# Layer 0 of a hybrid streaming encoder: the second block's norm behind the first block's gates, the third block's in front of its own

## Chip, cores and metric

The kernel runs on one NeuronCore of one Trainium2 chip. The metric is the device time of one execution in microseconds (us); lower is better. The runs before the change took 2411.01 to 2415.98 us, with a median of 2411.66 us over 3 runs.

## What is computed

Two layers of a chunk-causal encoder on 1024 prompt frames and 8 x 16 sample frames, together 1152 tokens of width 1024. Cut to what matters:

```
for l in range(2):
    h = rms_norm(x, norm1_g[l])
    q, k, v, a, b = split(h @ w_in[l]);  u = a * sigmoid(b)      # u: the "gates"
    A = sink_attention(rope(norm(q)), rope(norm(k)), v)          # a chunk of 64 reads up to 3 chunks
    C = silu(layer_norm(causal_depthwise_conv31(u)))
    x = x + concat(beta_a * A, beta_c * C) @ w_out[l]
    x = x + relu(rms_norm(x, norm2_g[l]) @ w_up[l])**2 @ w_down[l]
```

## The kernel before

**Blocks.** The tokens lie in three blocks of 384 columns (b = 0, 1, 2), stored with the width on the partitions: a block x is 8 tiles of 128 x 384, loaded by `load_x` (L187) in four DMAs. `rmsnorm` (L250, steps L255) squares x on ScalarE (L260), adds the squares on VectorE (L264, L265), sums over partitions on TensorE (L241), takes the reciprocal root on GpSimd (five short operations, L231 to L235), spreads it with TensorE (L247), and then scales x on VectorE (L275) and parts each value into a rounded half (ScalarE, L276) and a rest (VectorE, L277). The two halves are the tile pair `h`. Every product of a block reads its `h`.

**Products.** Each weight tile arrives as two DMAs `raw`, is rounded on ScalarE (L205) and split on GpSimd (L206), and goes through 24 matmuls of 128 x 384 (L213 to L215). `raw` has 4 buffers, the split weights `w` 6, the PSUM banks `g` of the products 3.

**Stages of layer 0.** `glu(l, b, h)` (L290) makes the gates of block b in eight products; L308 to L310 on ScalarE and L312 on GpSimd finish them. `make_qkv` (L356) makes queries, keys and values in six. `attention` gives a generator that makes one chunk of 64 queries at each step: scores on TensorE (L525), row maximum and its bookkeeping on VectorE (L492 to L502), exponentials (L533) and scaling (L541) on ScalarE, transposes (L550), copies out of PSUM (L551 ScalarE, L552 VectorE), products with the values (L560), and the output `ao` (L564 to L566). The transposes of a chunk and its output share a single PSUM bank `m`, the scores have one tile `s`. `conv` makes the depthwise convolution as 31 VectorE steps (L345, L347) for each of four channel tiles, and its tail (L647 to L665, L640, L641) gives `co`. Attention and convolution advance a little after each product (`tick`). `out(b)` (w_out) multiplies `ao` and `co` with the output weights, and needs all of both.

**What sets the order.** The program is written by hand in this order, and a scheduler then makes one fixed queue for each engine from it at build time, working on its own estimate of the times. On the chip each engine takes its queue strictly in order. Names like `x_573` carry a serial number that shifts by a constant where a tile is made earlier or later; tiles of block 3's norm are x_573, f_578 and following, h_607, h_608 in the kernel before, and x_2223, f_2228 and following, h_2257, h_2258 in the changed one.

Of the kernel before, what the change touches and what calls it, by code (L numbers as in the profile page):

```python
# [42 lines left out]
G1, G2, QG, KG = 0, 8, 16, 17  # L43
# [18 lines left out]
class Kernel:  # L62
# [951 lines left out]
    def run(self):  # L1014
        nc, tc, a = self.nc, self.tc, self.a
        pool = tc.tile_pool
        PS = bass.MemoryType.PSUM
        src = [a["x"][b] for b in range(NB)]
        early = ExitStack()
        self.fp = early.enter_context(pool(name="f0", bufs=1))  # L1020
        self.hp = early.enter_context(pool(name="hp0", bufs=1))
        self.aux = early.enter_context(pool(name="aux0", bufs=1, space=PS))
        x = [self.load_x(src[0])]
        self.load_consts()
        x.append(self.load_x(src[1]))
        h1 = [self.rmsnorm(x[b], 0, G1) for b in range(2)]
        for l in range(DEPTH):
            self.u, self.co, self.k, self.vb = [None] * NB, [None] * NB, [], []
            x, h, ao = [None] * NB, [None] * NB, [None] * NB
            fin = l == DEPTH - 1  # L1030
            nsrc = [a["y"][b] if fin else self.dp.tile([128, KT, BT], F32, tag=f"x{b}", name=f"xd{l}{b}") for b in range(NB)]
            kept = self.dp.tile([128, KT, BT], F32, tag=f"kept{l}", name=f"kept{l}")
            nh = []
            alone, pair, place, mix, conv, att = (t[l] for t in (ALONE, PAIR, PLACE, MIX, CONV, ATT))

            def blk(b, end=False, x=x, h=h, nsrc=nsrc, nh=nh, l=l, fin=fin):
                then = None if fin or not end else lambda: nh.append(self.rmsnorm(x[b], l + 1, G1))
                return x[b], h[b], nsrc[b] if end else None, then

            def attention(b, qf):  # L1040
                ao[b], g = self.attention(l, b, *qf)
                self.side("attention", g, att[b])

            def out(b):
                co = self.tail_of(b)
                x[b] = self.load_x(src[b], self.mark)
                self.w_out(l, x[b], ao[b], co)
                if b < NB - 1:
                    h[b] = self.rmsnorm(x[b], l, G2)

            with tc.tile_pool(name=f"ap{l}", bufs=1) as self.ap:
                self.mix = 0
                self.mix = mix[0]
                self.glu(l, 0, h1[0], conv)
                if l == 0:
                    for n in ("sk", "sv", "sc"):
                        self.after(nc.sync.dma_start(a[n + "o"], a[n + "old"]), self.mark)
                    h1.append(self.rmsnorm(self.load_x(src[2]), l, G1))
                attention(0, self.make_qkv(l, 0, h1[0]))
                if l:  # L1060
                    self.glu(l, 1, h1[1], conv)
                qf = self.make_qkv(l, 1, h1[1])
                self.finish("attention")
                attention(1, qf)
                if not l:
                    self.glu(l, 1, h1[1])
                    self.side("conv", self.conv(l, 1), conv[1])
                if l:
                    out(0)
                    self.flush()  # L1070
                    self.mix = 0
                    self.glu(l, 2, h1[2])
                else:
                    self.glu(l, 2, h1[2])
                    out(0)
                self.back, self.mix = self.feed_forward(l, range(alone), [blk(0)]), mix[1]
                qf = self.make_qkv(l, 2, h1[2])
                self.finish("attention")
                attention(2, qf)
                self.side("conv", self.conv(l, 2), conv[2])  # L1080
                out(1)
                self.flush()
                for _ in self.feed_forward(l, range(alone), [blk(1)], True):
                    pass
                for _ in self.feed_forward(l, range(alone, place), [blk(0), blk(1)]):
                    pass
                self.finish("attention")
            yp = ExitStack()
            self.yp = yp.enter_context(pool(name=f"yp{l}", bufs=1, side="right"))
            forms, three, fourth = self.pair_forms(h[0], h[1])  # L1090
            self.side("forms", three, FORMS[l])

            def firsts(l=l, fourth=fourth):
                self.finish("forms")
                self.side("forms", fourth, 1)

            self.back, self.mix = self.feed_forward(l, range(place, pair), [blk(b) for b in range(2)], then=firsts), mix[2]
            out(2)
            for i in range(0, KT, 4):
                nc.sync.dma_start(kept[:, i:i + 4], x[2][:, i:i + 4])  # L1100
            self.queue = self.quads(l, range(pair, NG))
            self.ahead = self.quad(next(self.queue))
            self.flush()
            self.finish("forms")
            self.mix = 0

            def second(x=x, h=h, l=l):
                x[2] = self.load_x(kept, self.mark)
                self.arena = [self.slot([4, 2, BT], F32, "f"), 0]
                for i, h[2] in enumerate(self.rmsnorm_steps(x[2], l, G2)):  # L1110
                    for _ in range((3, 3, 1)[i]):
                        yield
                self.arena = None

            early.close()
            self.aux = None
            with pool(name=f"xp{l}", bufs=1) as self.xp, pool(name=f"px{l}", bufs=1, space=PS) as self.px:
                self.ahead("sums")
                self.turn = 7
                then = second()  # L1120
                self.pair_feed(l, range(pair, NG), x, forms, then)
                for _ in then:
                    pass
            yp.close()
            early = ExitStack()
            self.fp = early.enter_context(pool(name=f"f{l + 1}", bufs=1))
            self.hp = early.enter_context(pool(name=f"hp{l + 1}", bufs=1))
            self.aux = early.enter_context(pool(name=f"aux{l + 1}", bufs=1, space=PS))
            for b in range(2):
                for i in range(0, KT, 4):  # L1130
                    nc.sync.dma_start(nsrc[b][:, i:i + 4], x[b][:, i:i + 4])
            if fin:
                with tc.tile_pool(name=f"fp{l}", bufs=NFW) as fp:
                    for _ in self.feed_forward(l, range(NG), [blk(2, True)], True, fp):
                        pass
            else:
                self.back = self.feed_forward(l, range(NG), [blk(2, True)])
                self.fill(FILL)
                nh += [self.rmsnorm(x[b], l + 1, G1) for b in range(2)]
            h1, src = nh, nsrc  # L1140
        early.close()
# [119 lines left out]
```

## Time and profile before

| what | value |
|---|---|
| median of 3 runs | 2411.66 us |
| profiled execution, its own time | 2407.56 us |
| span of its instructions | 2405.8 us |
| busy: TensorE (PE), its weight loads | 96 %, 94 % of the span |
| busy: VectorE (DVE), GpSimd (POOL), ScalarE (ACT) | 69 %, 64 %, 53 % |
| mean granted TensorE clock | 0.992 of 2.4 GHz |

The profile is of one execution, 4.1 us under the median of the runs. The shares are means over stages that have different limits. Layer 0 up to the first feed-forward product is about the first 345 us, and it is in this stretch that the change works.

### The profile page before, as it was taken

Reading aid. Unit: us, or ns where it says so; the run is one execution under the profiler, and the core shown is the slowest. Engines: PE = TensorE matmul, PEld = TensorE weight load, DVE = VectorE, ACT = ScalarE, POOL = GpSimd, SP = SyncE. Lnnn points to the kernel's source line nnn. Section 1 sums busy time; section 2 is a strip of 40 time slices with the busy share of each in tenths; the row PEclk is TensorE's granted clock in tenths of the full one; section 3 lists DMA queues with packets and bytes.
Section 4 is the critical chain, followed back from the end, with each engine's and each line's share of the span. In section 5 each row is a group of like instructions: output and inputs, shape, how many; then the busy total and the mean of one; then the engine's idle time right before and its main releaser. Section 6 shows DMA issues by size and latency. Waiting matters only on the chain.

```text
span 2405.8 us, 38983 instructions
## 1 busy us (share of the span) xinstructions
PE 2319.9 (96%) x13822; PEld 2254.8 (94%) x13822; DVE 1658.2 (69%) x2993; ACT 1270.5 (53%) x2732; POOL 1530.3 (64%) x1375
## 2 busy tenths in 40 slices
PE   6999898999999999999999999999999999999999
PEld 6898798999998999999999999999999899999999
DVE  4999887996368777686687764599834877752222
ACT  5467555555435555554566467466443555544442
POOL 5885566566467666766865776856445666676662
PEclk9999899999999999999999999999999999999999
DMA  5422433334332222544333344334333122244442
GB/s 179 139 92 93 122 96 110 111 107 138 110 97 78 68 71 80 164 122 134 101 119 108 114 155 134 128 105 124 97 101 118 55 70 75 84 162 136 132 127 75
DMA packets 164260, 266.49 MB, mean 111 GB/s; under 512 B 24753, under 2 KB 55729, under 8 KB 164017
## 3 DMA queue, kind: packets, MB, share of 16 engines
q1 hardware_dynamic: 164064, 264.01, 35.5%
q8 instruction: 108, 1.77, 0.3%
q14 instruction: 88, 0.71, 0.1%
HBM read 250.19 MB, written 16.05 MB: 111 GB/s over the span
## 4 chain that ended last, share of the span: by engine, by line
PE 76%; DVE 16%; POOL 3%; issue 2%; DMA 2%; ACT 2%; SPq 0%; DVEq 0%; POOLq 0%; ACTq 0%
PE g L715 14%; PE g L213 13%; PE g L215 13%; PE g L214 13%; DVE c L347 5%; PE x L998 4%; PE x L918 4%; PE g L998 3%; PE g L918 2%; PE m L715 2%; PE r L715 2%; POOL w L885 1%; PE c L715 1%; DMA A<-in_w 1%; PE s L525 1%
## 5 line engine op out<-in xcount | busy, mean ns | idle before, releaser
L206 POOL TENSOR_TENSOR w<-raw,w 128x512 fp32r<-128x512 f32 x728 | 965.6, 1336 | 592.3 <-ACT w L205 572.7
L205 ACT CAST w<-raw 128x512 fp32r<-128x512 f32 x728 | 445.6, 620 | 457.6 <-PE g L715 134.6
L213 PE MATMUL g<-h,w 128*128 128x384 f32 x1696 | 576.4, 340 | 7.2 <-ACT h L276 3.8
L214 PE MATMUL g<-h,w 128*128 128x384 f32 x1696 | 573.1, 338 | 1.1 <-DVE h L277 1.1
L215 PE MATMUL g<-h,w 128*128 128x384 f32 x1696 | 573.4, 338 | 0.0
L347 DVE SCALAR_TENSOR_TENSOR c<-u,vec,c 128x384 f32<-128x384 f32 (+1 forms) x960 | 498.5, 519 | 19.0
L715 PE MATMUL g<-hid,w 128*128 128x384 f32 x2304 | 431.2, 341 | 9.3 <-DVE x L717 6.3
L715 PEld LDWEIGHTS g<-hid,w 128*128 128x128 f32 x2304 | 399.6, 189 | 17.8 <-DVE x L717 10.8
L213 PEld LDWEIGHTS g<-h,w 128*128 128x128 f32 x1696 | 320.8, 189 | 11.4 <-ACT h L276 4.6
L214 PEld LDWEIGHTS g<-h,w 128*128 128x128 f32 x1696 | 320.6, 189 | 2.8 <-DVE h L277 2.0
L215 PEld LDWEIGHTS g<-h,w 128*128 128x128 f32 x1696 | 320.4, 189 | 0.7
L699 DVE TENSOR_TENSOR hid<-t,hid 128x384 fp32r<-128x384 f32 x128 | 106.3, 831 | 197.4 <-ACT hid L698 197.2
L885 POOL TENSOR_TENSOR w<-S,w 128x512 fp32r<-128x512 f32 x96 | 138.5, 1446 | 120.0 <-ACT w L884 119.7
L717 DVE TENSOR_TENSOR x<-x,g 128x384 f32<-128x384 f32 x240 | 129.8, 549 | 77.0 <-PE g L715 76.7
L696 ACT ACTIVATE t<-g 128x384 f32<-128x384 f32 x128 | 62.9, 491 | 143.7 <-PE g L215 142.5
L998 PE MATMUL x<-F,w 128*128 128x384 f32 x624 | 119.2, 336 | 3.4 <-DVE x L1001 2.4
L885 POOL TENSOR_TENSOR w<-raw,w 128x512 fp32r<-128x512 f32 x64 | 90.6, 1416 | 41.0 <-ACT w L884 39.7
L998 PEld LDWEIGHTS x<-F,w 128*128 128x128 f32 x624 | 109.4, 188 | 4.9 <-DVE x L1001 2.5
L998 PE MATMUL g<-F,w 128*128 128x384 f32 x528 | 108.3, 340 | 4.1 <-ACT F L807 1.4
L884 ACT CAST w<-S 128x512 fp32r<-128x512 f32 x96 | 59.7, 622 | 96.1 <-DVE S L871 51.1
L998 PEld LDWEIGHTS g<-F,w 128*128 128x128 f32 x528 | 92.6, 188 | 8.4 <-ACT F L807 2.7
L885 POOL TENSOR_TENSOR w<-A,w 128x512 fp32r<-128x512 f32 x64 | 87.0, 1364 | 18.6 <-ACT w L884 18.4
(227 smaller groups left out, 4016.8 us busy)
## 6 DMA issues: line engine op xcount, KB each, us to landing
raw<-in_w SPq DMA_DIRECT2D x792, 256.0 KB, 2.7
A<-in_w SPq DMA_DIRECT2D x64, 256.0 KB, 2.8
x<-in_x SPq DMA_DIRECT2D x24, 384.0 KB, 4.8
x<-xd SPq DMA_DIRECT2D x12, 384.0 KB, 5.2
kept<-x SPq DMA_DIRECT2D x4, 768.0 KB, 4.0
x<-kept SPq DMA_DIRECT2D x8, 384.0 KB, 4.7
xd<-x SPq DMA_DIRECT2D x4, 768.0 KB, 3.5
out_y<-x SPq DMA_DIRECT2D x4, 768.0 KB, 4.7
```

The costliest lines, as they stand in the source:

```text
L205: nc.scalar.copy(u[:, 0], raw)
L206: nc.gpsimd.tensor_tensor(out=u[:, 1], in0=raw, in1=u[:, 0].bitcast(F32), op=ALU.subtract)
L213: nc.tensor.matmul(ps, lhsT=u(0, k), rhs=h(0, k), start=k == 0, stop=False)
L214: nc.tensor.matmul(ps, lhsT=u(0, k), rhs=h(1, k), start=False, stop=False)
L215: self.pe = nc.tensor.matmul(ps, lhsT=u(1, k), rhs=h(0, k), start=False, stop=k == KT - 1)
L347: t = nc.vector.scalar_tensor_tensor(out=o, in0=src(k), scalar=w, in1=o, op0=ALU.mult, op1=ALU.add)
L699: nc.vector.tensor_tensor(out=hid[:, 1], in0=f, in1=hid[:, 0].bitcast(F32), op=ALU.subtract)
L715: self.pe = nc.tensor.matmul(ps, lhsT=u(p), rhs=hid[:, q], start=i == 0, stop=i == n - 1)
L717: nc.vector.tensor_tensor(out=x[:, m], in0=x[:, m], in1=ps, op=ALU.add)
L885: nc.gpsimd.tensor_tensor(out=u[:, 1], in0=f[n], in1=u[:, 0].bitcast(F32), op=ALU.subtract)
L918: nc.tensor.matmul(ps, lhsT=u[:, p, k], rhs=H[h](q, k), start=start and k == 0 and i == 0, stop=k == 3 and i == 2, skip_group_check=True)
L998: nc.tensor.matmul(o, lhsT=u[:, p, 2 * i + j], rhs=F(j, hn)[:, q], start=start and n == 0, stop=n == 5, skip_group_check=True)
```

## The change

Before, blocks 0 and 1 are loaded and normed at the very start, and block 2 is loaded and normed between block 0's gates and its queries. After, only block 0 is normed at the start; block 1 is loaded and normed between block 0's gates and its queries; and block 2 is loaded (its DMAs ordered behind the last sigmoid of block 1's gates) and normed right in front of its own gates. Nothing is added or left out.

```
@@ run @@
         x = [self.load_x(src[0])]
         self.load_consts()
-        x.append(self.load_x(src[1]))
-        h1 = [self.rmsnorm(x[b], 0, G1) for b in range(2)]
+        h1 = [self.rmsnorm(x[0], 0, G1)]
...
                 self.glu(l, 0, h1[0], conv)
                 if l == 0:
...
-                    h1.append(self.rmsnorm(self.load_x(src[2]), l, G1))
+                    h1.append(self.rmsnorm(self.load_x(src[1]), l, G1))
                 attention(0, self.make_qkv(l, 0, h1[0]))
...
                 else:
+                    h1.append(self.rmsnorm(self.load_x(src[2], self.mark), l, G1))
                     self.glu(l, 2, h1[2])
                     out(0)
```

**First place: GpSimd at the start of the program.** `s_118` to `s_122` before, and `s_113` to `s_117` after, are the reciprocal root of block 0's norm; the `w` are the first weights of its gates. Before:

```order
L231 TENSOR_TENSOR s_120<-s_118,half 128x3
L206 TENSOR_TENSOR w_216<-raw_215,w_216 128x512
L232 TENSOR_TENSOR s_121<-s_120,s_118 128x3
L206 TENSOR_TENSOR w_221<-raw_220,w_221 128x512
L206 TENSOR_TENSOR w_250<-raw_249,w_250 128x512
L233 TENSOR_TENSOR s_121<-s_121,s_120 128x3
L206 TENSOR_TENSOR w_255<-raw_254,w_255 128x512
L206 TENSOR_TENSOR w_305<-raw_304,w_305 128x512
L234 TENSOR_SCALAR s_121<-s_121 128x3
L206 TENSOR_TENSOR w_310<-raw_309,w_310 128x512
L235 TENSOR_TENSOR s_122<-s_121,s_120 128x3
```

After, on the same engine at the same place:

```order
L206 TENSOR_TENSOR w_160<-raw_159,w_160 128x512
L206 TENSOR_TENSOR w_165<-raw_164,w_165 128x512
L206 TENSOR_TENSOR w_194<-raw_193,w_194 128x512
L206 TENSOR_TENSOR w_199<-raw_198,w_199 128x512
L206 TENSOR_TENSOR w_249<-raw_248,w_249 128x512
L231 TENSOR_TENSOR s_115<-s_113,half 128x3
L206 TENSOR_TENSOR w_254<-raw_253,w_254 128x512
L232 TENSOR_TENSOR s_116<-s_115,s_113 128x3
L233 TENSOR_TENSOR s_116<-s_116,s_115 128x3
L234 TENSOR_SCALAR s_116<-s_116 128x3
L235 TENSOR_TENSOR s_117<-s_116,s_115 128x3
```

Six splits stand among the five root operations before; after, five of them stand ahead of the root and one inside it. In SyncE's queue, block 1's four load DMAs move from ahead of the first weight to behind the tenth.

**Second place: TensorE at the end of block 1's gates.** `g_2130` before, and `g_2074` after, is the last product of those gates; `g_2282` is the first product of block 2's gates. Before:

```order
L525 MATMUL s_1718<-k_854,q_631 128x192 x12
L214 MATMUL g_2130<-h_183,w_2171 128x384
L215 MATMUL g_2130<-h_182,w_2171 128x384
L213 MATMUL g_2130<-h_182,w_2171 128x384
L214 MATMUL g_2130<-h_183,w_2171 128x384
L215 MATMUL g_2130<-h_182,w_2171 128x384
L213 MATMUL g_2282<-h_607,w_2285 128x384
L214 MATMUL g_2282<-h_608,w_2285 128x384
L215 MATMUL g_2282<-h_607,w_2285 128x384
L213 MATMUL g_2282<-h_607,w_2285 128x384
```

After:

```order
L214 MATMUL g_2074<-h_552,w_2115 128x384
L215 MATMUL g_2074<-h_551,w_2115 128x384
L550 MATMUL m_1583<-cst,p_1555 128x128
L550 MATMUL m_1583<-cst,p_1556 128x128
L525 MATMUL s_1925<-k_798,q_981 128x128 x6
L525 MATMUL s_1925<-k_1302,q_981 128x64 x6
L525 MATMUL s_1925<-k_798,q_981 128x128 x6
L525 MATMUL s_1925<-k_1302,q_981 128x64
L560 MATMUL m_1583<-pt_1576,v_809 128x256 x6
L560 MATMUL m_1583<-pt_1584,v_891 128x256 x3
L525 MATMUL s_1925<-k_1302,q_981 128x64 x5
L550 MATMUL m_1635<-cst,p_1615 128x128
```

After, no product follows block 1's gates for 184 instructions: they are 96 of scores, 30 transposes, 45 with the values and 13 of norms, that is all six chunks of block 1's attention as far as their scores go. Only then comes `g_2282`. Before, these same instructions stand scattered between the products of block 2's gates and of `out(0)`. From the first addition of block 0's down-projection on (L717 into x_2764), the queues of the two kernels differ by exchanged neighbours alone, and from TensorE's instruction 2870 of 13494 on not at all.

**Third place: ScalarE, where block 2's norm stands after the change.** `p_2818` and `p_2819` are the exponentials of block 1's fifth chunk, `p_2621` those of its fourth:

```order
L260 ACTIVATE f_2230<-x_2223 128x768
L533 ACTIVATE p_2621,s_2628<-s_2607,s_2622,s_982 128x3x64 x2
L551 CAST pt_2203<-m_2202 128x256
L260 ACTIVATE f_2233<-x_2223 128x768
L541 ACTIVATE p_2620<-p_2620,s_2628 128x3x64 x2
L541 ACTIVATE p_2621<-p_2621,s_2628 128x3x64 x2
L260 ACTIVATE f_2236<-x_2223 128x768
L533 ACTIVATE p_2818,s_2826<-s_2805,s_2820,s_982 128x3x64 x2
L565 CAST ao_1722<-og_2217 128x4x64
L551 CAST pt_2486<-m_2485 128x512
...
L276 CAST h_2257<-f_2259 128x768
L276 CAST h_2257<-f_2264 128x768
```

Before, the same squares stand among block 0's last gate operations:

```order
L205 CAST w_693<-raw_692 128x512
L260 ACTIVATE f_578<-x_573 128x768
L308 COPY t_551<-g_480 128x384
L205 CAST w_698<-raw_697 128x512
L276 CAST h_182<-f_199 128x768
L205 CAST w_737<-raw_736 128x512
L260 ACTIVATE f_580<-x_573 128x768
```

The squares of block 2's norm now stand behind the exponentials of block 1's fourth chunk, and the halves `h` that its gates need behind the exponentials of the fifth.

## Rows read from the trace of the kernel before

**Rows 1.** Page, busy us (share of the span) and instructions of each engine.
```profile
PE 2319.9 (96%) x13822; PEld 2254.8 (94%) x13822; DVE 1658.2 (69%) x2993; ACT 1270.5 (53%) x2732; POOL 1530.3 (64%) x1375
```

**Rows 2.** Stretch: us, busy PE, PEld, DVE, ACT, POOL; granted clock, DMA share, GB/s.
```profile
61.00:134.00 73.00, 68.06 (x448) 64.45 (x447) 68.14 (x122) 34.61 (x73) 63.48 (x68) 0.93 0.42 136
182.00:230.00 48.00, 46.87 (x311) 44.14 (x310) 46.72 (x86) 32.63 (x89) 25.33 (x22) 1.00 0.30 94
230.00:286.00 56.00, 47.61 (x275) 44.50 (x274) 49.51 (x93) 33.84 (x80) 28.49 (x31) 0.91 0.46 130
286.00:349.00 63.00, 57.56 (x359) 54.59 (x357) 55.59 (x103) 33.51 (x73) 38.36 (x44) 0.92 0.29 89
```

**Rows 3.** Timeline of the start: start us, length us, instruction, idle before and releaser.
```profile
13.02 2.56 ACT L205 CAST w<-raw 128x512 fp32r<-128x512 f32 x4 [3.35 <-DMA raw<-in_w]
13.10 0.86 POOL L231 TENSOR_TENSOR s<-s,half 128x3 f32<-128x3 f32 x1 [10.23 <-DMA raw<-in_w]
13.93 1.26 POOL L206 TENSOR_TENSOR w<-raw,w 128x512 fp32r<-128x512 f32 x1
21.74 0.19 POOL L235 TENSOR_TENSOR s<-s,s 128x3 f32<-128x3 f32 x1
24.98 1.33 PE L213 MATMUL g<-h,w 128*128 128x384 f32 x3 [2.09 <-ACT h L276]
```

**Rows 4.** DMA issues of the first 30 us: what, queue, count, KB each, us to landing.
```profile
x<-in_x SPq DMA_DIRECT2D x8, 384.0 KB, 5.7
```

**Rows 5.** One microsecond of the start, columns as in rows 2.
```profile
11.00:12.00 1.00, 0.70 (x4) 0.70 (x4) 0.25 (x1) 0.00 (x0) 0.00 (x0) 1.00 1.00 377
```

**Rows 6.** TensorE's waits from 60 to 134 us: sum, times, longest.
```profile
PE r L418 <- DVE t L383: 2.1, 1, 2.1
PE g L213 <- DVE s L438: 1.8, 1, 1.8
```

**Rows 7.** Four microseconds behind the first of these waits, columns as in rows 2.
```profile
100.00:104.00 4.00, 2.16 (x8) 2.11 (x8) 3.94 (x9) 1.32 (x3) 2.31 (x3) 0.50 0.09 32
```

**Rows 8.** Timeline of VectorE, 84 to 98 us.
```profile
85.31 2.18 DVE L275 SCALAR_TENSOR_TENSOR f<-x,vec,r 128x384 f32<-128x384 f32 x4
...
96.92 0.54 DVE L383 TENSOR_TENSOR t<-t,r 128x384 f32<-128x384 f32 x1
```

**Rows 9.** Timeline: TensorE's first gate product of block 2, and a chunk on ScalarE.
```profile
182.46 0.34 PE L213 MATMUL g<-h,w 128*128 128x384 f32 x1
...
188.78 0.51 ACT L533 ACTIVATE p<-s,s,s 128x192 f32<-128x192 f32 x1 [2.71 <-DVE s L495]
...
192.36 1.50 ACT L541 ACTIVATE p<-p,s 128x192 f32<-128x192 f32 x4 [0.24 <-DVE s L502]
```

**Rows 10.** ScalarE by form, 100 to 340 us: count, busy us, mean ns, idle before.
```profile
L533 ACT ACTIVATE p<-s,s,s 128x192 f32<-128x192 f32 x40 | 20.3, 512 | 19.9 <-DVE s L495 17.5 <-PE m L550 2.5
L551 ACT CAST pt<-m 128x512 fp32r<-128x512 f32 x11 | 6.4, 583 | 0.1
L260 ACT ACTIVATE f<-x 128x768 f32<-128x768 f32 x4 | 3.4, 845 | 0.0
L665 ACT ACTIVATE u<-u,vec 128x384 f32<-128x384 f32 x4 | 2.5, 696 | 0.4 <-DVE u L662 0.4
L665 ACT ACT_TABLE_LOAD x1 | 1.3, 1283 | 0.0
```

**Rows 11.** TensorE and VectorE by form, 182 to 349 us.
```profile
L560 PE MATMUL m<-pt,v 128*128 128x256 f32 x81 | 12.1, 295 | 0.2 <-DVE pt L552 0.2
...
L525 PE MATMUL s<-k,q 64*128 64x192 f32 x48 | 5.3, 330 | 0.0
...
L492 DVE TENSOR_REDUCE s<-s 128x4 f32<-128x768 f32 x7 | 6.6, 949 | 0.0
```

**Rows 12.** TensorE's longest wait from 134 to 345 us.
```profile
PE g L213 <- ACT co L640: 5.1, 1, 5.1
```

**Rows 13.** Timeline of VectorE: the instruction from which on the queues agree.
```profile
345.44 0.54 DVE L717 TENSOR_TENSOR x<-x,g 128x384 f32<-128x384 f32 x1
```

More of the change, by code (lines that the diff above doesn't have):

```diff
@@ L1024, in run @@
         self.load_consts()
-        x.append(self.load_x(src[1]))
-        h1 = [self.rmsnorm(x[b], 0, G1) for b in range(2)]
+        h1 = [self.rmsnorm(x[0], 0, G1)]
         for l in range(DEPTH):
@@ L1057, in run @@
                         self.after(nc.sync.dma_start(a[n + "o"], a[n + "old"]), self.mark)
-                    h1.append(self.rmsnorm(self.load_x(src[2]), l, G1))
+                    h1.append(self.rmsnorm(self.load_x(src[1]), l, G1))
                 attention(0, self.make_qkv(l, 0, h1[0]))
@@ L1073, in run @@
                 else:
+                    h1.append(self.rmsnorm(self.load_x(src[2], self.mark), l, G1))
                     self.glu(l, 2, h1[2])
```

## The prediction

> **What bounds the kernel now.** I read the page first: TensorE is busy 96 % of the span and its weight loads 94 % [rows 1], so for most of the kernel only TensorE's lost time can be won. Then I cut the part that the change touches into stretches and took, for each, TensorE's lost time as length less busy time x granted clock, since a matmul at half the clock counts as busy. From 61 to 134 us (queries, keys and values of blocks 0 and 1) 73 - 68.06 x 0.93 = 9.7 us are lost; from 182 to 230 us (block 2's gates) 1.1; from 230 to 286 us (`out(0)`) 56 - 47.61 x 0.91 = 12.7; from 286 to 349 us 63 - 57.56 x 0.92 = 10.0 [rows 2]. The reader should see that in all of these VectorE is nearly as busy as TensorE: 68.14 of 73, 46.72 of 48, 49.51 of 56, 55.59 of 63. It is a stage with two limits, and it runs well only where attention and convolution have products of another block beside them. Then I went to the lost time itself: the timeline of the start, the waits, and the granted clock behind a wait. Before 25 us there is one more hole: TensorE's first product starts at 24.98 [rows 3].
>
> **What the change does, part by part.** The work is the same to the last instruction. So every cost or gain is waiting that goes or comes, and I follow TensorE's time to the place from which the queues agree again, the addition at 345.44 [rows 13], about where TensorE reaches 349 us.
>
> *Start.* Before, block 1's four loads of 384 KB lie ahead of the first weight [rows 4]. The DMA engines are full at 377 GB/s [rows 5], so 4 x 0.393 MB take 4.2 us, and the first weight, rounded at 13.02 [rows 3], can be rounded at 8.8. GpSimd then splits from about 9.5. Before, its root began at 13.10 and, with six splits among its steps, ended at 21.93 [rows 3]. After, five splits of 1.26 us come first (to 15.8), then the root's first step of 0.86, a split, and four short steps of 0.19: 18.7. That is 3.2 us earlier; I take **-3** (bounds -2 and -4). Block 1's loads now start when the sixth split has freed its buffer, about 18 us, and land in some 6 us [rows 4], about when ScalarE first wants them behind block 0's last halves. This move costs nothing; if the loads were 2 us late, ScalarE's squares would be, and those have block 0's remaining gates as cover.
>
> *Queries, keys and values.* Block 2's norm held VectorE between 85.31 and 96.92, right ahead of L383, the norm of block 0's keys [rows 8]. TensorE waited 2.1 us for L383 and then 1.8 us for L438 behind it [rows 6], and the granted clock stood at 0.50, that is 1.2 GHz, right behind the first wait [rows 7]: some 3 us more. Block 1's norm now stands there instead of two norms, so VectorE reaches L383 with some 11 us less work done (the stretch 85.31 to 96.92). I take 7 of the 9.7 us: **-7** (bounds 0 and -9.7).
>
> *The hole in front of block 2's gates.* Now block 2's norm starts only when block 1's gates are done, and its squares and halves stand on ScalarE behind the exponentials of block 1's fourth and fifth chunk. Products before 182.46 [rows 9] have nothing to follow them but attention, chunk after chunk. I estimate the hole from block 1's last gate product to block 2's first. From the first gate product of block 2 to the exponentials of block 0's last chunk before: 188.78 - 182.46 = 6.3 [rows 9]; I take the same lead. One chunk on ScalarE, first exponential to last scaling: 192.36 + 1.50 - 188.78 = 5.1 [rows 9]; the next chunk's scores, 12 at 0.11 (5.3 / 48), its maximum, 0.95 [rows 11], and a copy out of PSUM, 0.58 [rows 10], come between: 7.9, say 8 a chunk. From those exponentials to the halves of block 2's `h` there are five chunks: 40. The tail of block 0's convolution falls into the same place on ScalarE with two table loads of 1.3 and its SiLU of 2.5, and block 2's squares take 3.4 [rows 10]: 8.5. One more for the first halves: 6.3 + 40 + 8.5 + 1 = 56 us. In them TensorE does 184 small instructions that lay behind 182.46 before, at 0.11 to 0.15 each (5.3 / 48, 12.1 / 81 [rows 11]): 20 to 27, I take 22. So the hole costs 56 - 22 = **+34**. From below, ScalarE's own work alone is 24 x 0.51 + 20 x 0.375 + 6 x 0.58 + 2.5 + 2.6 + 3.4 = 32 [rows 9, 10], with the lead 38, which makes +16. From above, waits let the clock fall to half, as after 2.1 us in rows 7; if half of the 22 us of small matmuls lie on the chain at twice their time, the hole is 67 and the cost +45. Behind TensorE wait its gate products, and with them ScalarE's L308 to L310, the convolution of block 1 (ordered behind block 2's products) and `out(0)`.
>
> *Behind the hole.* Block 1's attention is then over, and block 0's `co`, for which TensorE waited 5.1 us in `out(0)` [rows 12], is long ready. So the 12.7 us lost from 230 to 286 mostly go; of the 10.0 from 286 to 349, where `out(0)`'s own norm is waited for, I let 4 go. Against that, the halves of `h` come one by one while VectorE still has a softmax to do, and the clock must rise again: +4 (an estimate: four microseconds at 0.50 as in [rows 7] cost 2, and I let the halves cost as much). Together 11 + 4 - 4: **-11** (bounds -19 and -4).
>
> Sum: -3 - 7 + 34 - 11 = **+13 us**. The profiled execution took 2407.56 us of device time around its span of 2405.8, so it would take 2420.6. That execution is 4.1 us under the median of the runs; on the median the forecast is 2411.66 + 13 = 2424.7, about **2425 us**.
>
> **A rule against the trace.** The rows show that products and attention beside each other fill TensorE to 46.87 of 48 us [rows 2], and the change takes them apart. The Trainium skill, Perfetto Trace Analysis, section Optimization Strategy, says that where the most contended engine changes between regimes, interleaving the regimes may help; it speaks against this change. By that rule the sum is a loss; without it, by the section Identifying the Most-Contended Engine of the same page, the busiest engine is the one to improve, and an unchanged TensorE at 96 % would leave the sum at 0. The second reading is a rival of its own below.
>
> **The rivals.**
> - *Slower as above* (the forecast), chance 0.62.
> - *Faster: ScalarE fills the hole.* If the six chunks overlap so well that ScalarE is never idle, the hole is 38 us and costs +16; with -9 from the queries and -11 behind the hole, the sum is -3 - 9 + 16 - 11 = -7: 2405 us. It decides below a hole of 43 us (22 + 3 + 7 + 11). For it speaks that two chunks are always in work; against it that scores have one tile, transposes one bank, so each chunk waits for the one ahead, and that ScalarE stood idle 19.9 us ahead of 40 exponentials [rows 10]. Chance 0.13.
> - *No change: waits only move.* Attention's dependencies cost TensorE the same wherever they stand, 33.5 us between 61 and 349 as now (9.7 + 1.1 + 12.7 + 10.0 [rows 2]): 2412 us. The hole's 34 us would have to be just these; but not all of them come from attention. Chance 0.11.
> - *Much slower: hole at half clock.* Hole 67 us, nothing won in the queries, losses behind it down by only 9: -3 + 45 - 9 = +33: 2445 us. Chance 0.14.
> - That block 2's norm is made early all the same is excluded by ScalarE's queue, where its squares stand behind a fourth chunk that needs block 1's queries.
>
> The unknown terms give the likeliest case a range of 2417 to 2436; with the neighbours the range is **2409 to 2443**. A measurement of this kernel tells 0.2 %, 4.8 us, from no change. Faster by more: 0.13. Within: 0.13 (the third case, and a little of the first). Slower: 0.74.
>
> **What would show it.** Right: the first product at about 22 us; no wait for L383 near 95; block 1's gates done near 172; then TensorE busy less than half of the time for 50 to 60 us, with the clock at 0.5 in parts, and ScalarE's exponentials following each other at about 8 us; block 2's gates from about 228; no wait for `co` in `out(0)`; the L717 at about 358. Wrong: a hole under 43 us; a hole that GpSimd or the load of block 2 ends instead of ScalarE; or losses between 290 and 400 us that vanish because TensorE comes later while VectorE does not.

## The result: 21 us slower, and where the profile after shows them

The changed kernel takes 2432.16 us (median of 6 runs, 2428.48 to 2434.87), the kernel before, run on the same chip, 2410.98 us (6 runs, 2407.15 to 2415.98): a ratio of 1.0088, 95 % interval 1.0073 to 1.0103. The forecast was 2425 us with a range of 2409 to 2443. So the direction held and the range held, but the loss is 21 us where 13 were forecast. Between the two profiled executions it is 25.4 us (2432.95 against 2407.56). The page of the changed kernel:

```profile
PE 2331.0 (96%) x13822; PEld 2266.5 (93%) x13822; DVE 1651.7 (68%) x2993; ACT 1273.4 (52%) x2732; POOL 1530.1 (63%) x1375
```

The shares are those of [rows 1] to within a point: the page alone shows nothing. The first three stretches of [rows 2] do:

```profile
61.00:134.00 73.00, 68.96 (x457) 64.77 (x455) 62.79 (x123) 33.14 (x73) 64.10 (x72) 0.93 0.41 134
182.00:230.00 48.00, 30.04 (x152) 23.96 (x152) 24.77 (x58) 33.09 (x90) 6.41 (x10) 0.54 0.19 59
230.00:286.00 56.00, 51.16 (x289) 49.27 (x290) 43.08 (x81) 33.46 (x80) 28.47 (x32) 0.85 0.32 93
```

In the second row TensorE is busy 30 of 48 us at a granted clock of 0.54. That is the hole. TensorE's timeline shows its edges and its beat, in one row for each chunk's scores:

```profile
183.57 0.34 PE L215 MATMUL g<-h,w 128*128 128x384 f32 x1
...
189.31 2.34 PE L525 MATMUL s<-k,q 64*128 64x128 f32 x19 [1.24 <-ACT p L533]
...
198.81 2.61 PE L525 MATMUL s<-k,q 64*128 64x64 f32 x22 [1.03 <-ACT p L533]
...
208.90 1.60 PE L525 MATMUL s<-k,q 64*128 64x192 f32 x12 [1.24 <-ACT p L533]
...
218.69 1.60 PE L525 MATMUL s<-k,q 64*128 64x192 f32 x12 [0.97 <-ACT p L533]
...
232.16 1.59 PE L525 MATMUL s<-k,q 64*128 64x192 f32 x12 [1.04 <-ACT p L533]
...
243.06 1.59 PE L525 MATMUL s<-k,q 64*128 64x192 f32 x12 [0.97 <-ACT p L533]
244.59 1.33 PE L213 MATMUL g<-h,w 128*128 128x384 f32 x3
```

Block 1's gates end at 183.9 us and block 2's begin at 244.6: a hole of 60.7 us. The chunks follow each other at 9.5, 10.1, 9.8, 13.5 and 10.9 us. The long one holds block 0's convolution tail, which ScalarE's timeline shows without a pause:

```profile
219.16 1.28 ACT L665 ACT_TABLE_LOAD   x1 [0.26 <-DVE s L501]
220.46 2.50 ACT L665 ACTIVATE u<-u,vec 128x384 f32<-128x384 f32 x4
222.86 1.48 ACT L541 ACTIVATE p<-p,s 128x192 f32<-128x192 f32 x4
224.25 2.11 ACT L640 ACTIVATE co<-u,vec 128x384 fp32r<-128x384 f32 x4
226.38 1.28 ACT L533 ACT_TABLE_LOAD   x1
```

I cut the time anew at the hole's edges, up to the same point of the feed-forward in both kernels (its first matmul at 349.3 us before lies at 377.0 after). First the kernel before, in two stretches, then the changed one in three:

```profile
0.00:182.40 182.40, 153.48 (x985) 145.38 (x986) 144.38 (x260) 99.60 (x218) 136.52 (x147) 0.97 0.42 136
182.40:349.30 166.90, 151.94 (x940) 143.13 (x939) 151.75 (x279) 99.86 (x240) 92.09 (x96) 0.94 0.35 104
```

```profile
0.00:183.90 183.90, 153.22 (x976) 144.31 (x976) 146.66 (x260) 94.92 (x214) 134.18 (x143) 0.97 0.38 127
183.90:244.60 60.70, 38.27 (x195) 30.68 (x194) 33.25 (x78) 42.13 (x114) 8.51 (x17) 0.52 0.15 48
244.60:377.00 132.40, 125.68 (x755) 123.25 (x754) 115.33 (x199) 64.52 (x129) 82.05 (x83) 0.95 0.38 119
```

Two readings come from these five rows. TensorE's lost time (length less busy x clock) behind 182.4 was 166.9 - 151.94 x 0.94 = 24.1 us. After, the hole loses 60.7 - 38.27 x 0.52 = 40.8 and the rest 132.4 - 125.68 x 0.95 = 13.0. So the hole gave back 11.1 us of the 40.8 that it lost. These figures are good to a few us only: busy time x clock, which is the same work in both kernels, adds up to 291.7 us in the two rows before and to 287.9 in the three after. And VectorE does the same work up to the common point, 144.38 + 151.75 = 296.1 us before and 295.2 after, but is idle for 349.3 - 296.1 = 53.2 us before and 81.8 after. In the hole itself it is busy 33 of 61 us: the taps (single steps) of block 1's convolution (L347) are ordered in the program behind products that don't come.

### The profile page after: what moved, and what is told of

It is laid out like the page before. It is cut to its first block, busy times and chain, and to the rows that moved or that the text cites. A ratio compares the mean times of both kernels' runs of the same rounds, so it can differ in the third digit from the quotient of the medians.

```text
span 2431.1 us, 38994 instructions
## 1 busy us (share of the span) xinstructions
PE 2331.0 (96%) x13822; PEld 2266.5 (93%) x13822; DVE 1651.7 (68%) x2993; ACT 1273.4 (52%) x2732; POOL 1530.1 (63%) x1375
## 4 chain that ended last, share of the span: by engine, by line
PE 77%; DVE 13%; POOL 4%; issue 2%; ACT 2%; DMA 2%; SPq 0%; DVEq 0%; POOLq 0%; ACTq 0%
PE g L715 14%; PE g L213 13%; PE g L214 13%; PE g L215 13%; PE x L918 4%; PE x L998 4%; DVE c L347 3%; PE g L918 3%; PE g L998 3%; PE m L715 2%; PE r L715 2%; POOL w L885 1%; PE c L715 1%; PE s L525 1%; PE m L560 1%
## 5 line engine op out<-in xcount | busy, mean ns | idle before, releaser
L347 DVE SCALAR_TENSOR_TENSOR c<-u,vec,c 128x384 f32<-128x384 f32 (+1 forms) x960 | 498.4, 519 | 20.2
L717 DVE TENSOR_TENSOR x<-x,g 128x384 f32<-128x384 f32 x240 | 129.9, 548 | 78.1 <-PE g L715 77.8
```

Source lines behind the costliest of these rows:

```text
L347: t = nc.vector.scalar_tensor_tensor(out=o, in0=src(k), scalar=w, in1=o, op0=ALU.mult, op1=ALU.add)
L717: nc.vector.tensor_tensor(out=x[:, m], in0=x[:, m], in1=ps, op=ALU.add)
```

## The experiments

Theory: the loss is the hole, and what it costs is the time that TensorE loses in it less what `out(0)` and the stretch up to the feed-forward would have lost anyway. Rivals: block 1's late norm; block 2's late load; TensorE's slow clock in the hole. The times of all kernels, each against the kernel before on the same chip ("hole" is the stretch from block 1's last gate product to block 2's first; 0 where no such stretch is in the queue):

| run | hole, us | median, us | ratio to before, 95 % interval |
|---|---|---|---|
| changed kernel | 60.7 | 2432.16 | 1.0088 (1.0073 to 1.0103) |
| second_half | 60.0 | 2429.2 | 1.0073 (1.0061 to 1.0086) |
| load_early | 51.2 | 2423.82 | 1.0065 (1.0051 to 1.0079) |
| behind_queries1 | 29.3 | 2405.08 | 0.9972 (0.9960 to 0.9984) |
| queries1_start1 | 30.0 | 2409.19 | 0.9981 (0.9973 to 0.9990) |
| behind_queries0 | 0 | 2405.43 | 0.9976 (0.9964 to 0.9988) |
| queries0_start1 | 0 | 2405.6 | 0.9970 (0.9956 to 0.9983) |
| both_behind_gates0 | 0 | 2413.28 | 1.0001 (0.9991 to 1.0011) |
| behind_queries1_v4 | 0 | 2420.21 | 1.0028 (1.0018 to 1.0038) |
| no_table_load | 57.3 | 2427.79 | 1.0057 (1.0042 to 1.0073) |
| one_product | 55.1 | 2431.3 | 1.0076 (1.0061 to 1.0092) |
| short_conv | 57.9 | 2424.96 | 1.0053 (1.0039 to 1.0067) |
| filled_hole | 79.2 | 2457.01 | 1.0183 (1.0169 to 1.0197) |

### Each half of the change alone

**second_half**, against the changed kernel:

```
-        h1 = [self.rmsnorm(x[0], 0, G1)]
+        x.append(self.load_x(src[1]))
+        h1 = [self.rmsnorm(x[b], 0, G1) for b in range(2)]
...
-                    h1.append(self.rmsnorm(self.load_x(src[1]), l, G1))
```

> Only the second half of the change: blocks 0 and 1 are loaded and normed at the start as before, block 2 in front of its own gates; TensorE's queue again has 184 instructions between the last gate product of block 1 and the first of block 2. Theory A (the hole makes the loss; the end of block 1's gates is set by the sum of VectorE's work up to there, which is 158 us in both kernels): a hole of 58 to 64 us, no wait for L383 near 95, block 1's gates done at 182 to 187 all the same, and 2428 to 2438 us, that is the changed kernel's time or 2 to 4 us more for the later first product (about 25 us). Theory B (the loss comes from block 1's late norm, whose load and work crowd block 1's gates): block 1's gates done near 172 to 175 and 2415 to 2422 us.

The hole and the time are as theory A had them. The end of block 1's gates is not: it comes at 178.4 us, between the two theories. The first stretch and the hole:

```profile
0.00:178.40 178.40, 150.93 (x976) 142.54 (x976) 138.49 (x250) 95.58 (x214) 134.02 (x143) 0.99 0.41 130
178.40:238.40 60.00, 35.48 (x193) 28.19 (x193) 39.26 (x88) 41.88 (x114) 8.47 (x17) 0.58 0.17 53
```

VectorE has done 138.5 us of work by then, not 158 as I had written (that was the sum with overlaps; the rows above give 144.4 and 146.7 for the two kernels). The second half by itself brings the end of block 1's gates forward by 4.0 us (178.4 against 182.4), though the first product comes as late as before the change. The first half, added to it, moves that end back by 5.5 us, to 183.9, though it starts the products 2.1 us earlier. The first half of the change is thus no gain of its own: with the hole there, it costs 3 us by the medians, and the intervals of the two ratios overlap.

**both_behind_gates0**, against the changed kernel: the first half alone.

```
                     h1.append(self.rmsnorm(self.load_x(src[1]), l, G1))
+                    h1.append(self.rmsnorm(self.load_x(src[2]), l, G1))
...
-                    h1.append(self.rmsnorm(self.load_x(src[2], self.mark), l, G1))
```

> The first half of the change alone: block 0 normed at the start, blocks 1 and 2 both loaded and normed between block 0's gates and its queries; no hole in TensorE's queue (at most 33 instructions without a product). Theory A: no hole, so the loss of 21 us is gone; the first product at 23 us gives 2 us, the two norms in front of block 1's queries cost the wait for L383 at least as before (2 to 6 us lost near 95); 2407 to 2414 us. Theory B (block 1's late norm costs by itself): 2418 to 2428 us.

Without the hole the loss is gone, as theory A says (ratio 1.0001). The price of two norms in one place is larger than I wrote. TensorE's timeline between block 0's queries and block 1's:

```profile
98.98 0.90 PE L247 MATMUL r<-cst,s 128*128 128x128 f32 x3 [5.56 <-POOL s L235]
107.72 1.55 PE L382 MATMUL r<-cst,s 128*64 128x128 f32 x12 [7.84 <-DVE f L275]
110.88 1.17 PE L418 MATMUL r<-cst,t 64*64 64x64 f32 x12 [1.61 <-DVE t L383]
...
116.00 0.69 PE L213 MATMUL g<-h,w 128*128 128x384 f32 x1 [2.58 <-DVE s L438]
```

These four waits are 17.6 us. At the common point the kernel is 10 us behind the one before (359.6 us), at the end 1.6 by the medians and 6.0 between the profiled executions.

### How long a hole may be

**behind_queries0** and **behind_queries1** put block 2's norm one and two stages later than that, still ahead of block 1's gates (the line of block 2's norm in front of its own gates is taken out in both):

```
+                if not l:
+                    h1.append(self.rmsnorm(self.load_x(src[2]), l, G1))
                 qf = self.make_qkv(l, 1, h1[1])
```

```
                 qf = self.make_qkv(l, 1, h1[1])
+                if not l:
+                    h1.append(self.rmsnorm(self.load_x(src[2]), l, G1))
```

> As the changed kernel, but block 2 is loaded and normed between block 0's and block 1's queries. No hole in the queue before block 2's gates (33 instructions without a product at most). Theory A (VectorE's sum sets the end of block 1's gates): they end at 178 to 183, the whole 2404 to 2411 us. Theory C (the 7 us in front of L383 are won for good once block 2's norm is out of there and no hole follows): block 1's gates done by 176, 2398 to 2404 us.

> As the changed kernel, but block 2 is loaded and normed between block 1's queries and block 1's gates. TensorE's queue has 107 instructions without a product in front of block 2's gates, where the changed kernel has 186. Theory A (the hole costs what its attention chunks take on the chain ScalarE, VectorE, TensorE): a hole of 30 to 40 us with the clock at 0.5 in most of it, 2413 to 2424 us. Rival (the hole costs only once block 2's squares wait behind the fourth chunk; with the norm in front, the products start when block 1's gates are done): no loss, 2405 to 2411 us.

behind_queries0 went as theory A says in time, though block 1's gates end only at 193.2 us, outside its 178 to 183. What was lost ahead of that end is regained behind it: 156.3 us from there to the common point, where the kernel before takes 166.9. behind_queries1 is the surprise: the hole came as theory A has it, 29.3 us, and cost nothing, which was the rival's time. Its hole and what follows, up to the common point:

```profile
181.40:210.70 29.30, 19.15 (x112) 16.13 (x111) 12.67 (x37) 17.65 (x55) 7.93 (x13) 0.65 0.09 28
210.70:351.10 140.40, 136.43 (x837) 130.96 (x838) 131.42 (x239) 85.31 (x185) 87.80 (x90) 0.96 0.40 116
```

The hole loses 29.3 - 19.15 x 0.65 = 16.9 us and the rest 140.4 - 136.43 x 0.96 = 9.4: together 26.3, against 24.1 before the change. TensorE's wait of 5.1 us for `co` in `out(0)` [rows 12] is gone there as well. But there are only 24 us to be given back, and in every kernel with a hole here 9 to 14 us stay lost behind it; so a hole that loses 17 us is nearly free, and of one that loses 41 most is paid.

**load_early** lies between: the load of block 2 alone stands earlier.

```
+                    x2 = self.load_x(src[2])
                     self.glu(l, 1, h1[1])
...
-                    h1.append(self.rmsnorm(self.load_x(src[2], self.mark), l, G1))
+                    h1.append(self.rmsnorm(x2, l, G1))
```

> The changed kernel, but block 2's four loads stand ahead of block 1's gates in the program; its norm stays in front of its own gates. TensorE's queue has 159 instructions without a product there, between the 107 that cost nothing (a hole of 29 us, 2405 us) and the 186 of the changed kernel (61 us, 2432 us). Theory A (what a hole has above some 30 us is paid nearly in full, 0.85 us for each, and the load itself is of no account): by the count of instructions the hole is 45 to 55 us and the time 2418 to 2428 us. Rival (it is the late load that makes the change slow): a hole under 35 us, 2403 to 2410 us.

Theory A, on all counts: 51.2 us and 2423.82. Waiting for the load is not the cause: with the load issued at 137 us most of the hole and of the loss stay. What its place does is to let the scheduler put ScalarE's squares one chunk earlier in the queue, and the hole is shorter by that chunk. From 29.3 to 51.2 us the time rises by 18.7 us (22 by the ratios), from there to 60.7 by 8 (6 by the ratios).

**queries1_start1** and **queries0_start1** are the same two places for block 2's norm, with block 1 loaded and normed at the start as before the change (the edit of second_half).

> Blocks 0 and 1 loaded and normed at the start as before the change; block 2 loaded and normed between block 1's queries and block 1's gates (107 instructions without a product in front of block 2's gates). Theory A (up to the first feed-forward product the time is VectorE's summed work, about 295 us, and its idle time; work that fills VectorE's gaps beside block 0's gates is free): the first product is 2 us later, block 1's gates end at 174 to 178 instead of 181, and the time is 2399 to 2405 us, as good as or up to 5 us better than with block 1's norm behind block 0's gates (2405 us). Rival (the gain of that kernel came from the earlier first product and the free queries of block 0): 2405 to 2411 us.

> Blocks 0 and 1 loaded and normed at the start; block 2 loaded and normed between block 0's and block 1's queries; 37 instructions without a product at most. Theory A: block 1's gates end at 184 to 190 instead of 193, and the time is 2400 to 2406 us. Rival: 2405 to 2411 us, as before the change or as the kernel with block 1's norm behind block 0's gates (2405 us).

The four kernels' intervals overlap, so where block 1's norm stands decides nothing that these runs can tell; theory A's further gain is not shown. All four are faster than both kernels of this study, by 0.2 to 0.3 % than the one before. In the profiled executions that gain isn't made where the norms stand: the four reach the common point at 348.3 to 351.1 us, the kernel before at 349.3. At the addition L717 that the kernel before reaches at 569.5 us they are 3.1 to 7.8 us ahead. All kernels of the table but behind_queries1_v4 gain 1.4 to 9.2 us on the kernel before between the addition of [rows 13] and that one, the changed kernel too (28.6 us behind, then 24.1). Why is not shown.

### What makes the hole, and what its length hangs on

**behind_queries1_v4** takes behind_queries1 and one number:

```
-            vb = self.ap.tile([128, 2, 3, 128], F32R, tag="v", name=self.nm("v"), bufs=3)
+            vb = self.ap.tile([128, 2, 3, 128], F32R, tag="v", name=self.nm("v"), bufs=4)
```

> As the kernel with block 2's norm between block 1's queries and block 1's gates (a hole of 29 us with 107 instructions), but the split values v get a fourth buffer. In that kernel TensorE's sum for the norm (L241) stands behind the transposes of block 1's values (L418), which wait for a buffer of v that only block 1's third chunk frees; with four buffers the queue has no more than 33 instructions without a product. Theory A (this wait makes the hole): block 2's gates start within 2 us of the end of block 1's gates, and the time is 2395 to 2404 us. Rival (the attention's waits come back wherever it stands): no hole, but 5 to 10 us more lost in block 2's gates and out(0), and 2403 to 2409 us.

In behind_queries1 the rows that end the hole are these, of GpSimd, ScalarE and TensorE:

```profile
200.11 0.74 POOL L414 MEMSET v<- 128x768 f32 x1 [13.45 <-PE m L560]
```

```profile
200.88 0.31 ACT L420 CAST v<-r 64x192 fp32r<-64x192 f32 x1 [2.44 <-POOL v L414]
```

```profile
203.22 0.83 PE L241 MATMUL r<-cst,f 128*128 128x1 f32 x6 [0.17 <-DVE v L421]
```

The third buffer of v comes free when a chunk has multiplied with it (L560); then the transposed values leave the PSUM bank r, and only then can the norm's sum (L241) use that bank. With a fourth buffer the hole is gone, so the mechanism is shown. But the kernel is slower, 2420.21 us, and both expected times missed. Up to the common point it is 4.0 us behind the kernel before: between 178.6 and 353.3 us TensorE waits for the transposed halves 5.3 us in three places and for seven other things 0.5 to 2 us each:

```profile
PE m L550 <- DVE pt L552: 5.3, 3, 2.9
```

The rest of its loss of 7.5 us comes behind that point, and what the fourth buffer does there stays open. The Trainium skill, Perfetto Trace Analysis, section Optimization Strategy, says that a gap on the busiest engine that keeps repeating can mean too little buffer space for the next tile. Here the gap was a single one, a missing buffer did make it, and the buffer that closed it made the kernel slower: 1.0028 against 0.9972.

The last four take the changed kernel and change what is done in the hole or ahead of it. **one_product**, with `parts` in the place of the three pairs in the scores' and the values' loops:

```
+        parts = ((0, 0),) if l == 0 and b == 1 else ((0, 0), (0, 1), (1, 0))
```

> The changed kernel, but the attention of layer 0's block 1 multiplies only the rounded halves (one product of three in the scores and with the values; the corrections are left out). Theory A (in the hole TensorE's small matmuls at half the clock are on the chain, some 4.5 us in each chunk's 9.8): the hole of 61 us shrinks by 2.5 to 3 us a chunk, to 44 to 50 us, and the time to 2412 to 2424 us. Rival (ScalarE and VectorE alone set the pace of the chunks): the hole stays at 56 to 61 us, and 2425 to 2432 us.

This leaves out the corrections, two of three products. The hole is 55.1 us, just outside the rival's range, and the time 2431.3 is the rival's. With 75 matmuls fewer in it (120 against 195) the hole is 5.6 us shorter; the median is 0.9 us lower, 2.9 by the ratios, whose intervals overlap.

```profile
183.10:238.20 55.10, 28.31 (x120) 21.05 (x120) 33.63 (x79) 42.69 (x117) 8.16 (x17) 0.55 0.16 52
```

TensorE is busy 10 us less than in the changed kernel's hole, VectorE (33.6) and ScalarE (42.7) as long as there. These matmuls are thus worth about 1 us of a chunk's 10: TensorE's slow matmuls are a small part of the chunks' pace.

**no_table_load**:

```
-            nc.scalar.activation(y[:, ct], y[:, ct], AF.Silu, bias=self.v(l, LNB + ct), scale=self.v(l, LNG + ct))
+            nc.scalar.activation(y[:, ct], y[:, ct], AF.Silu if l or b else AF.Tanh, bias=self.v(l, LNB + ct), scale=self.v(l, LNG + ct))
```

> The changed kernel with tanh in the place of SiLU in block 0's convolution of layer 0, which spares ScalarE's two table loads of 1.3 us there; nothing else in the five queues changes. The prediction booked 8.5 us of the hole for these loads, the SiLU and block 2's squares. Theory A (ScalarE is what the chunks wait for in this place: 219 to 228 us without a pause): the hole shrinks by 2 to 3 us, from 60.9 to 58 to 59, and the time falls by 1 to 3 us against the changed kernel's 2432. Rival (other waits fill it): hole and time as they were, 60 to 61 us and 2431 to 2434.

Block 0's convolution gets tanh in the place of its SiLU. Theory A's direction, and more than it said: the hole is 57.3 us, 3.4 shorter and not 2 to 3, and the time 2427.79, 4.4 us lower by the medians (7 by the ratios) and not 1 to 3. Two table loads of 1.28 us fewer shortened the hole by 3.4 us, so here ScalarE is waited for; what the time gained beyond the hole is not traced.

**short_conv**:

```
-            for k in range(CW):
+            taps = CW - (4 if ct < 2 else 3) if l == b == 0 else CW
+            for k in range(taps):
```

> The changed kernel, but block 0's convolution in layer 0 leaves out its last 14 taps of 124 (8.7 us of VectorE's work, as many L347 as the changed kernel has more than the one before ahead of the end of block 1's gates). Theory A (VectorE's summed work sets when block 1's gates end): they end at 175 to 179 instead of 183.9, and the time is 4 to 9 us under the changed kernel's, 2423 to 2428 us. Rival (the attention's own chain sets it): they end at 181 to 184, and the time stays within 3 us, 2429 to 2435 us.

Theory A in the time, 2424.96; the end of block 1's gates, 180.1 us, lies between the two. VectorE has done 5.4 us less by that end than in the changed kernel:

```profile
0.00:180.10 180.10, 152.01 (x980) 143.36 (x980) 141.28 (x253) 98.75 (x222) 130.57 (x139) 0.98 0.41 130
```

So of 8.7 us of VectorE's work 3.8 come off block 1's gates and 7.2 off the whole (8 by the ratios). By the end of block 1's gates VectorE has worked 138.5 us in second_half, 141.3 here, 144.4 before the change and 146.7 after, and been idle 39.9, 38.8, 38.0 and 37.2 us: where more work stands ahead of that end, it comes later, though not by the full amount.

**filled_hole**, behind the scores of each chunk:

```
+            if l == 0 and b == 1:
+                for _ in range(32):
+                    nc.tensor.matmul(s[:, 0, 384:], lhsT=self.k[0][:, 0, :128], rhs=self.k[0][:, 0, :128], start=True, stop=True)
```

> The changed kernel with 32 more matmuls of 128 columns behind the scores of each chunk of layer 0's block 1; their results go into unused columns and nobody reads them. Theory A (the clock stays at 0.5 in the hole because TensorE has too little to do): with them the granted clock in the hole rises above 0.7, the chunks follow each other at 8 to 9 us instead of 9.8 in spite of the added work, and the hole is 50 to 60 us. Rival (the clock does not rise): the added 3.4 us of matmuls at 0.5 stand on the chain of each chunk, the hole is 70 to 80 us and the time 2440 to 2450 us.

The rival in the hole and the clock: the hole grows to 79.2 us and the clock stays down. The time, 2457.01 us, lies above even the rival's 2440 to 2450:

```profile
181.80:261.00 79.20, 69.39 (x343) 63.90 (x343) 33.60 (x75) 40.34 (x105) 8.19 (x17) 0.51 0.11 37
```

Here the added work lengthened the chain and the clock did not rise. No run had the same hole at full clock, so what the clock alone costs there is not measured; one_product's small gain only suggests that it is little.

## Why the prediction was right, and what was mis-sized

It named the right thing, a hole at the right place that attention fills and ScalarE's queue ends, and rightly let most of what it loses be paid. Term by term:

**Start, -3.** It was -2.0, the lower bound: the first product at 22.96 us against 24.98 [rows 3]. GpSimd's splits began at 9.70 as forecast (9.5), but the root ended at 19.9 instead of 18.7: the five splits took 7.2 us, not 6.3, and the short steps behind them 1.0, not 0.8:

```profile
9.70 7.18 POOL L206 TENSOR_TENSOR w<-raw,w 128x512 fp32r<-128x512 f32 x5 [6.83 <-DMA raw<-in_w]
...
19.72 0.19 POOL L235 TENSOR_TENSOR s<-s,s 128x3 f32<-128x3 f32 x1
```

**Queries, -7: this is the step that failed.** The wait for L383 [rows 6] did go; TensorE's longest waits from 61 to 134 us are now:

```profile
PE s L525 <- ACT q L452: 1.9, 1, 1.9
PE g L213 <- DVE s L438: 1.5, 2, 1.1
```

By block 1's queries the gain stood (its third product starts 4.4 us earlier beyond the start's 2.0). But "Block 1's gates done near 172" was wrong, they ended at 183.9, 1.5 us later than before. The gain was lost inside block 1's gates, where TensorE now waits for VectorE's steps of block 0's attention. Its waits for VectorE's steps L552 and L564 from 134 us to the end of these gates, before and then after:

```profile
PE m L550 <- DVE pt L552: 0.7, 1, 0.7
```

```profile
PE m L560 <- DVE pt L552: 2.0, 1, 2.0
PE m L550 <- DVE og L564: 1.6, 1, 1.6
PE m L550 <- DVE pt L552: 1.5, 1, 1.5
```

I had taken 11 us out of VectorE's queue and put nothing in their place. (The stretch that I read them from, 85.31 to 96.92, also holds five taps of the convolution, 3.1 us; up to the end of block 1's gates VectorE's steps of one norm come to 14 us.) VectorE's groups ahead of that end, before and after, show what came:

```profile
L347 DVE SCALAR_TENSOR_TENSOR c<-u,vec,c 128x384 f32<-128x384 f32 x106 | 65.5, 618 | 1.9
```

```profile
L347 DVE SCALAR_TENSOR_TENSOR c<-u,vec,c 128x384 f32<-128x384 f32 x120 | 74.2, 618 | 2.5
```

Fourteen more taps of block 0's convolution, 8.7 us, moved forward into the gap, and the first two steps of its tail (L647, L648) with 2.6, so VectorE had 146.7 us of work there instead of 144.4. The row for it was in the order of the kernels and I read only the places around the norms. The taps are part of the cause and not all of it: without fourteen taps (short_conv) the gates end at 180.1, without block 1's norm in the new place (second_half) at 178.4, and neither reaches 172. This term came out at +3.5 instead of -7: 10.5 us off, the largest of the errors (the others are 1.0, 4.7 and 0.1).

**Hole, +34.** It was 60.7 - 22 = +38.7, with the forecast's 22 us for the work done in it (38.27 x 0.52 in the row above is 19.9). ScalarE's exponentials of block 0's last chunk and of block 1's fifth, and the first halves of block 2's `h`:

```profile
184.93 0.51 ACT L533 ACTIVATE p<-s,s,s 128x192 f32<-128x192 f32 x1 [1.65 <-DVE s L495]
...
236.97 0.51 ACT L533 ACTIVATE p<-s,s,s 128x192 f32<-128x192 f32 x1 [1.75 <-DVE s L495]
...
243.16 1.60 ACT L276 CAST h<-f 128x768 fp32r<-128x768 f32 x2
```

The lead was 1.0 us, not 6.3. The five chunks took 52.0, tail included, where I had 40 + 8.5: by the scores' rows the first three beats were 9.8 and not 8, and the tail and block 2's squares, priced at 8.5, lengthened the other two by 4.8 together. From the fifth to the halves it was 6.2 and to the product 1.4 more, where I had 1. So the length came out within 5 us partly by luck, since the short lead and the cheap tail cancel most of the longer beat and the longer end. I had priced a chunk with its matmuls at full clock; at 0.5 its value products alone take 2.3 us. By one_product the slow matmuls are worth some 1 us a chunk. TensorE's longest waits in the hole show hand-overs between ScalarE, VectorE and TensorE; that the rest of the longer beat lies there is argued from them and not tested:

```profile
PE m L550 <- DVE pt L552: 11.2, 3, 6.3
PE s L525 <- ACT p L533: 6.5, 6, 1.2
```

**Behind the hole, -11.** It was -11.1 (24.1 less 13.0 above). There is no wait for `co` in out(0), as forecast. The right size within what these rows can tell, and near the most that any hole here gave back (14.7 in behind_queries1).

**Sum.** -2.0 + 3.5 + 38.7 - 11.1 = 29.1 at the common point, 1.4 above the 27.7 measured, which is within the few us that the lost times are good to; VectorE's addition of [rows 13] comes at 374.01 instead of the forecast 358:

```profile
374.01 0.54 DVE L717 TENSOR_TENSOR x<-x,g 128x384 f32<-128x384 f32 x1
```

By 567 us, where TensorE's queues have become the same, the loss is 24.1 us, and it ends at 25.3. The forecast had nothing given back so late; I did not trace these 4 us to single waits, and all other kernels here but behind_queries1_v4 gain on the one before there too. At the common point the forecast was some 15 us too low, at the end 12. Two of the signs that it named failed with the terms: TensorE was busy 63 % of the hole and not less than half, and the exponentials came at 10 us and not at 8.

**The rivals.** "ScalarE fills the hole" fell: ScalarE is busy 42 of 60.7 us. "Waits only move" fell for this hole, but up to the common point it is nearly what happens in one half as long. "Hole at half clock" had the clock (0.52) and rightly won nothing in the queries; its hole of 67 us was 6 too long and gave back 2 too little. Of the two sections of the Trainium skill, Perfetto Trace Analysis, that were weighed, the trace agrees with Optimization Strategy: two regimes that were interleaved were taken apart, and the time rose. In behind_queries1, where less of them is taken apart, it did not (0.9972). An unchanged busy share of 96 % for TensorE said nothing about it. The Trainium skill, Perfetto Trace Analysis, section Identifying the Most-Contended Engine, judges TensorE by the busy share of its weight loads, among others, and not by that of its matmuls. The weight loads took 94 % before and 93 % after, and said as little.

## What to carry to other kernels

When a step leaves a full engine's queue, look up what the scheduler puts in its place before booking the gain: here 11.3 us of convolution and its tail took up most of what a norm had left. A hole without products is not priced by its length but by the time lost in it against the time that is lost behind it anyway, and that second sum is a ceiling on what can come back (24 us here: 29 us of hole were free, 51 and 61 were not). So place a norm early enough that little is left between its product and the stage before, and don't expect that closing every hole is a gain: behind_queries1 kept one of 29 us and was faster than both_behind_gates0 and behind_queries1_v4, which have none.

## What was not expected of the hardware

In filled_hole TensorE was busy 69.39 of 79.2 us and the granted clock was 0.51 all the same. The stretches below show it busy without a pause from 242 us on, the clock at 0.50 (1.2 GHz) until about 265, 4 us after block 2's products had begun, and then at 0.99, that is 2.4 GHz:

```profile
242.00:252.00 10.00, 10.00 (x50) 9.67 (x51) 6.47 (x14) 5.05 (x15) 1.65 (x3) 0.50 0.00 0
252.00:262.00 10.00, 10.00 (x53) 9.83 (x50) 5.96 (x11) 3.60 (x8) 0.96 (x5) 0.50 0.00 0
...
263.00:265.00 2.00, 2.00 (x9) 2.00 (x9) 2.00 (x5) 0.83 (x1) 0.00 (x0) 0.50 0.00 0
265.00:267.00 2.00, 2.00 (x13) 2.00 (x12) 1.33 (x4) 0.28 (x1) 0.00 (x0) 0.99 0.00 0
```

So in this run the clock stayed at its lower level through 19 us in which TensorE was busy with small matmuls alone, and rose some 4 us into the products. Why it rose there is not shown.
